# A hybrid decoder trunk: the GLU's first output block moved into the steps of the state-space layer, and its output weights stored without delay 0

## The chip, the cores and the metric

The kernel runs on 1 core of one Trainium2 chip. The metric is the device time of one execution in microseconds; the kernel before took 2366.81 us (median of 3 runs, 2366.6 to 2368.81).

## What is computed

Two layers, each followed by a dense SwiGLU network, on 16 meta tokens and 256 tokens of width 2048, all in float32. The change touches the second layer, a diagonal complex state-space layer ("S5") and the gated linear unit (GLU) behind it:

```python
def s5_mixer(u, ...):                     # u: (1, 272, 2048), 128 groups of 16 channels, 64 complex states each
    ...                                   # lb = exp(lambda*dt), bb = b scaled for the step
    bu = einsum('blgh,gph->blgp', ug, bb)
    x = associative_scan(x[t] = lb * x[t-1] + bu[t])
    y = einsum('blgp,ghp->blgh', x_re, c_re) - einsum('blgp,ghp->blgh', x_im, c_im) + d_skip * u
    g = gelu(y)
    return (g @ w_glu1) * sigmoid(g @ w_glu2)      # both weights 2048 x 2048
```

## The kernel before, in words

**Products.** A float32 product is made of three matmuls with rounded operands: the weight is split into `whi` (a copy on ACT, line 102) and `wlo` (a subtraction on DVE, line 109), the activation into `xh` and `xl`, and TensorE adds whi·xh, whi·xl and wlo·xh (`mm3`, lines 297 to 299). The class `Weights` holds the whole program's weights as one list of chunks in the order of their use. `next()` hands out a chunk and calls `pump()`, which keeps the splits up to three chunks ahead (`ahead = SA = 3`; there are `WB = 4` buffers for each part) and starts the transfers of raw chunks four ahead of the last low part (`RB = 4`, line 96, on SP's queue). A raw chunk's buffer comes free only with the low part of the chunk that was in it.

**The state-space layer.** The sequence of 272 tokens is cut into 34 pieces of T = 8 tokens. While the first dense network runs on TensorE, matrices for each of the 16 tiles of 128 channels are prepared on the other engines and written to memory: `scr[k]` (input weights, rotations and, from column `CW0` on, the output weights `wide["c"]` for the delays 0 to 8) and `taps[k]`/`toep[k]`. Each transfer of the output weights takes all nine delays; `f_y` uses the last eight, `wv = ...[:, :, 16:]`.

Then come steps, i = -1 to 23, written out by `s5_step(i)` (line 1335). In a step each stage f works on tile k = i - lag:

```python
stages = [(f_load2, 2), (f_load, -1), (f_mod, 2), (f_c, 1), (f_g3, 8), (f_g2, 7), (f_u, -1),
          (f_g1, 6), (f_scan, 3), (f_yt, 5), (f_y, 4)]
```

`f_load` and `f_load2` start three transfers (tiles `w`, `w2`, named w too in the trace, and `kt`), `f_u` scales the input, `f_c` is the matmul into `x`, `f_mod` rotates it (`rc`, `rs_`, `z`), `f_scan` scans and rotates back (`v`, `xp`), `f_y` holds the matmuls into `y`, `f_yt` transposes it (`yy`), and `f_g1`, `f_g2`, `f_g3` are the GELU, whose results are `xh[:, k]` and `xl[:, k]`, the GLU's input for channel tile k. Every engine takes its instructions in the order written.

Steps -1 to 17 run on their own. Before step 15 one `W.pump()` splits one chunk ahead. The last six steps, 18 to 23, are put into the queue that `tick()` serves after each weight chunk, between the chunks of the GLU's first block.

**The GLU.** The 16 output tiles are made in blocks of 3, 3, 3, 3, 2 and 2 (`GLU_BLOCKS`). A chunk holds two input tiles 2c and 2c+1 for one of the two weights (i = 0: w_glu2, i = 1: w_glu1) and a block's output columns; 16 chunks make a block, and each output tile needs 6 matmuls of 256 columns per chunk. A block has one PSUM bank per output tile and weight. `th` is the sigmoid's tanh; `gate` multiplies; `osq` gathers squares for the norm that follows. After the first block the PSUM and SBUF of the steps are given back.

Of the kernel before, what the change touches and what calls it, by code (L numbers as in the profile page):

```python
# [10 lines left out]
F32 = mybir.dt.float32  # L11
# [20 lines left out]
T = 8  # L32
# [108 lines left out]
def trunk(  # L141
# [5 lines left out]
    nc = tc.nc  # L147
# [56 lines left out]
    plan_ffn(0)  # L204

    GLU_ORDER = [(c, i) for c in range(6) for i in range(2)] + [(6, 0), (7, 0), (6, 1), (7, 1)]
    for a, b in GLU_BLOCKS:
        for c, i in GLU_ORDER:
            W.add(rows((s5_w_glu2, s5_w_glu1)[i][0])[:, 2 * c:2 * c + 2, a * P:b * P], (2, (b - a) * P))
    plan_ffn(1)  # L210

# [13 lines left out]
    xh = keep.tile([P, KT, NT], F32R, name="xh")  # L225
    xl = keep.tile([P, KT, NT], F32R, name="xl")
# [33 lines left out]
    psm = ps_scope.enter_context(tc.tile_pool(name="psm", bufs=3, space=PSUM))  # L260
# [6 lines left out]
    def bank():  # L267
        return psm.tile([P, 512], F32, tag="mm", name="mm")
# [416 lines left out]
    osq = Squares(KT)  # L685
# [5 lines left out]
    ps2_scope = ExitStack()  # L691
    psm = ps2_scope.enter_context(tc.tile_pool(name="psm2", bufs=8, space=PSUM))
# [114 lines left out]
    pr = par_scope.enter_context(tc.tile_pool(name="pr", bufs=1))  # L807
    XW0, EW0 = 0, 1024
    CW0 = EW0 + 8 * NCP
    SCR = CW0 + 8 * 16 * (T + 1)  # L810
    scr = [dram.tile([P, SCR], F32, name=f"scr{k}") for k in range(KT)]

    ZB = 2 * T - 1
# [34 lines left out]
    M_, A_, S_ = ALU.mult, ALU.add, ALU.subtract  # L848
# [161 lines left out]
    def par_tile(k):  # L1010
        q = slice(4 * k, 4 * k + 4)
        d = loaded.setdefault(k, {})
# [110 lines left out]
        def store():  # L1123
            w = scr[k]
            nc.sync.dma_start(out=w[:, EW0:CW0], in_=d["e"].rearrange("p i q c -> p (i q c)"))
            nc.sync.dma_start(out=w[:, CW0:], in_=wide["c"].rearrange("p i q n h -> p (i q n h)"))

        loads[k], spreads[k] = load, spread_k

# [23 lines left out]
    osq = ffn(m, Sandwich(m, 0, 1, osq, (0, 2), NT), NT)  # L1153
# [8 lines left out]
    sp_scope = ExitStack()  # L1162
    sp = sp_scope.enter_context(tc.tile_pool(name="sp", bufs=2))
    sps_scope = ExitStack()
    sps = sps_scope.enter_context(tc.tile_pool(name="sps", bufs=1, space=PSUM))
    spx_scope = ExitStack()
    spx = spx_scope.enter_context(tc.tile_pool(name="spx", bufs=3, space=PSUM))

    d0 = [sp.tile([P, 4, NC], F32, name=f"d0{a}", bufs=1) for a in range(2)]
    for a in range(2):  # L1170
# [6 lines left out]
        td[k] = {"w": w}  # L1177

    def f_load2(k):
        w = sp.tile([P, SCR - CW0], F32, tag="w2", name="w2", bufs=3)  # L1180
        nc.sync.dma_start(out=w, in_=scr[k][:, CW0:])
        kt = td[k]["kt"] = sp.tile([P, T, 8, 16], F32, tag="kt", name="kt", bufs=3)
        v = toep[k].rearrange("t n -> (t n)")[:P * KL].rearrange("(r n) -> r n", r=P)
        nc.sync.dma_start(out=kt.rearrange("r t j h -> r (t j h)"), in_=v[:, (T - 1) * P:ZB * P])
        td[k]["w2"] = w
# [47 lines left out]
    def f_y(k):  # L1233

        d = td[k]
        ps = d["ps"] = sps.tile([P, 2, 512], F32, tag="y", name="y")
        wv = d["w2"].rearrange("p (a n) -> p a n", a=8)[:, :, 16:]
        kv = d["kt"].rearrange("p t j h -> p j t h")
        for g in range(2):
            for j in range(4):  # L1240
                nc.tensor.matmul(ps[32 * j:32 * j + 32, g, :P].rearrange("c (t h) -> c t h", t=T), d["U"][:, 2 * j + g, CM:], kv[:, 2 * j + g], start=True, stop=False)
        for g in range(2):
            r = slice(64 * g, 64 * g + 64)
            for i in range(2):
                for j in range(4):
                    nc.tensor.matmul(ps[32 * j:32 * j + 32, g, :P], d["xp"][r, i, j, CM:], wv[r, 4 * i + j], start=False, stop=(i == 1))
# [30 lines left out]
    for k in range(2):  # L1277
        f_load2(k)
# [4 lines left out]
    hs = {}  # L1283

    def turn(k):

        if k % 4 == 0:
            if k == 8:

                v = sp.tile([P, SCR - CW0], F32, tag="w2", name="hs", bufs=3)[:, :4 * NT]  # L1290
                hs[2] = v.rearrange("p (s k c) -> p s k c", s=T, k=4)
            else:
                hs[k // 4] = sp.tile([P, T, 4, NC], F32, tag="hs", name="hs")
        nc.scalar.copy(hs[k // 4][:, :, k % 4], hT[:, k].rearrange("p (c s) -> p s c", s=T))
# [6 lines left out]
    def read_u(g):  # L1301
        nc.sync.dma_start(out=m_flat[:, 4 * NT * g:4 * NT * (g + 1)], in_=ub[g])

    for k in range(KT + 2):
# [14 lines left out]
        if k == KT + 1:  # L1319
# [34 lines left out]
    ps2_scope = ExitStack()
    mr = m[:, :, :NREAL]

    osq = Squares(KT, cols=NREAL)
    ths = {}
    for a, b in GLU_BLOCKS:
        n = b - a  # L1360
        p2 = [bank()[:, :NREAL] for _ in range(n)]
        p1 = [bank()[:, :NREAL] for _ in range(n)]
        now = a == 0 or b == KT
        if b == KT:
            drain()

        def gate(o, a=a, p1=p1):
            tt(mr[:, a + o], p1[o], ths[a][:, o], M_)
            osq.add(mr[:, a + o])
        for c, i in GLU_ORDER:  # L1370
            hi, lo = W.next()
            if c == 7 and i == 1:
                ts(th[:, :n], th[:, :n], 0.5, 0.5, M_, A_)
                if b == KT:
                    warm(AF.Sqrt)
            for o in range(n):
                for k in range(2):
                    kt = 2 * c + k
                    mm3((p2, p1)[i][o], hi[:, k, o * P:(o + 1) * P], lo[:, k, o * P:(o + 1) * P],
                        xh[:, kt, :NREAL], xl[:, kt, :NREAL], kt == 0, kt == KT - 1)  # L1380
                if c == 7 and i == 1 and now:
                    gate(o)
            if c == 7 and i == 0:
                if a == 0:
                    th = sp.tile([P, SCR - CW0], F32, tag="w2", name="th", bufs=3)[:, :3 * NREAL].rearrange("p (o n) -> p o n", o=3)
                else:
                    th = sg.tile([P, 3, NREAL], F32, tag="th", name="th")
                ths[a] = th
# [5 lines left out]
        if a == 0:
            drain()
            psg_scope.close()
            sps_scope.close()
            sp_scope.close()
            sg = ctx.enter_context(tc.tile_pool(name="sg", bufs=2))
            psm = ps2_scope.enter_context(tc.tile_pool(name="psm3", bufs=8, space=PSUM))  # L1400
# [116 lines left out]
```

## Time and profile before

| | |
|---|---|
| runs | 2366.6, 2366.81, 2368.81 us; median 2366.81 |
| the profiled execution | 2366.55 us, of which the span from the first to the last instruction is 2364.6 us |
| busy, share of the span | PE 97%, DVE 60%, ACT 44%, POOL 26% |
| chain that ended last | PE 90%, DVE 5%, DMA, POOL, ACT and issue 1% each |
| mean granted TensorE clock | 0.977 of 2.4 GHz |
| transferred | 463.02 MB, mean 196 GB/s |

PE is busy through nearly the whole span. The page cuts the span into 40 slices of 59 us: in all but a few, PE is at nine tenths and the clock at full. The steps of the state-space layer lie in slices 23 and 24 (counted from 1).

### The profile page before, as it was taken

The numbers are of one execution on the slowest core, as the hardware profiler recorded it, in microseconds if no ns is written. First come the engines' busy times: TensorE is split into PE (matmuls) and PEld (weight loads), VectorE is DVE, ScalarE is ACT, GpSimd is POOL, SyncE is SP. The second block draws the span as 40 slices with busy tenths as digits, with TensorE's granted clock in tenths as the row PEclk, the third lists the DMA queues.
The fourth block names the chain that finished last, engine by engine and source line by source line (L and its number), as shares of the span: only waits on it lengthen the run. The fifth ranks groups of instructions, "written<-read, shape, count | busy, mean of one in ns | idle before, by whom it ended". The sixth has DMA issues, their size and how long they took to land.

```text
span 2364.6 us, 46794 instructions
## 1 busy us (share of the span) xinstructions
PE 2301.9 (97%) x18838; PEld 2207.0 (93%) x18838; DVE 1409.7 (60%) x2056; ACT 1043.6 (44%) x1582; POOL 611.9 (26%) x811
## 2 busy tenths in 40 slices
PE   8999999999999999999999789999999999999998
PEld 7999999999999999999999569998998999989996
DVE  6555556585755666656755695558555465545565
ACT  5434444553443443333444554446444444434443
POOL 2000001148665667547402350105000000000002
PEclk9999999999999999999999759999999999999999
DMA  6555555456777777777765885555665666655654
GB/s 172 143 152 153 155 151 171 139 155 189 245 235 227 237 228 245 229 229 218 255 212 166 295 312 179 184 176 147 182 201 202 183 184 178 205 184 177 193 192 156
DMA packets 391548, 463.02 MB, mean 196 GB/s; under 512 B 68596, under 2 KB 323092, under 8 KB 391188
## 3 DMA queue, kind: packets, MB, share of 16 engines
q1 hardware_dynamic: 391104, 459.97, 62.9%
q8 instruction: 147, 2.41, 0.4%
q14 instruction: 69, 0.57, 0.1%
q10 hardware_dynamic: 228, 0.08, 0.0%
HBM read 432.37 MB, written 43.32 MB: 201 GB/s over the span
## 4 chain that ended last, share of the span: by engine, by line
PE 90%; DVE 5%; DMA 1%; POOL 1%; ACT 1%; issue 1%; SPq 0%; DVEq 0%; POOLq 0%; ACTq 0%
PE mm L297 23%; PE mm L299 23%; PE mm L298 23%; PE mm L776 5%; PE mm L1443 3%; PE mm L1444 3%; PE mm L1442 3%; DVE wlo L109 1%; PE mm L754 1%; DVE v L1226 1%; PE mm L1062 1%; PE mm L761 1%; PE mm L1079 0%; DMA w<-scr 0%; POOL ct L843 0%
## 5 line engine op out<-in xcount | busy, mean ns | idle before, releaser
L109 DVE TENSOR_TENSOR wlo<-raw,whi 128x768 fp32r<-128x768 f32 (+2 forms) x891 | 945.7, 1074 | 505.2 <-ACT whi L102 497.8
L102 ACT CAST whi<-raw 128x768 fp32r<-128x768 f32 (+2 forms) x891 | 774.1, 884 | 829.1 <-PE mm L298 455.0
L299 PE MATMUL mm<-xh,wlo 128*128 128x272 f32 (+1 forms) x3544 | 1015.7, 287 | 5.5 <-DVE wlo L109 5.5
L297 PE MATMUL mm<-xh,whi 128*128 128x272 f32 (+1 forms) x3544 | 1020.2, 288 | 0.6 <-DVE m L843 0.6
L298 PE MATMUL mm<-xl,whi 128*128 128x272 f32 (+1 forms) x3544 | 1010.0, 285 | 0.0
L299 PEld LDWEIGHTS mm<-xh,wlo 128*128 128x128 f32 x3544 | 670.0, 189 | 7.6 <-DVE wlo L109 7.5
L297 PEld LDWEIGHTS mm<-xh,whi 128*128 128x128 f32 x3544 | 671.3, 189 | 5.3 <-issue 2.8
L298 PEld LDWEIGHTS mm<-xl,whi 128*128 128x128 f32 x3544 | 670.0, 189 | 0.0
L297 PE MATMUL mm<-ah,whi 128*128 128x272 f32 x944 | 274.1, 290 | 0.5 <-ACT m L678 0.5
L299 PE MATMUL mm<-ah,wlo 128*128 128x272 f32 x944 | 273.5, 290 | 0.0
L298 PE MATMUL mm<-al,whi 128*128 128x272 f32 x944 | 271.9, 288 | 0.0
L843 POOL TENSOR_TENSOR m<-m,gb 128x512 f32<-128x512 f32 x8 | 12.1, 1511 | 710.2 <-ACT mm L1456 693.9
L297 PEld LDWEIGHTS mm<-ah,whi 128*128 128x128 f32 x944 | 177.8, 188 | 1.6 <-ACT whi L102 0.8
L299 PEld LDWEIGHTS mm<-ah,wlo 128*128 128x128 f32 x944 | 178.1, 189 | 0.1
L298 PEld LDWEIGHTS mm<-al,whi 128*128 128x128 f32 x944 | 178.2, 189 | 0.0
L314 POOL TENSOR_TENSOR sqacc<-sqacc,sq 128x272 f32<-128x272 f32 (+1 forms) x81 | 85.3, 1053 | 243.3 <-ACT sq L309 241.5
L1443 PE MATMUL mm<-wlo,ah 128*128 128x512 f32 x352 | 137.4, 390 | 1.0 <-DVE wlo L109 1.0
L1442 PE MATMUL mm<-whi,ah 128*128 128x512 f32 x352 | 138.0, 392 | 0.0
L1444 PE MATMUL mm<-whi,al 128*128 128x512 f32 x352 | 137.3, 390 | 0.0
L843 POOL TENSOR_TENSOR bc<-ct,ct 128x64 f32<-128x64 f32 (+2 forms) x128 | 91.3, 733 | 73.1 <-PE mm L1079 69.3
L785 DVE TENSOR_TENSOR gs<-mm,r 128x272 f32<-128x272 f32 (+1 forms) x82 | 35.6, 434 | 107.2 <-PE mm L299 107.2
L582 POOL TENSOR_TENSOR z<-c,x 128x272 f32<-128x272 f32 x8 | 6.3, 783 | 289.8 <-DVE x L575 192.8
(437 smaller groups left out, 2411.4 us busy)
## 6 DMA issues: line engine op xcount, KB each, us to landing
raw<-in_ffn_w_gate_dram SPq DMA_DIRECT2D x224, 384.0 KB, 3.8
raw<-in_ffn_w_up_dram SPq DMA_DIRECT2D x224, 384.0 KB, 4.1
raw<-in_ffn_w_down_dram SPq DMA_DIRECT2D x168, 512.0 KB, 4.8
raw<-in_ab_w_in_dram SPq DMA_DIRECT2D x90, 512.0 KB, 4.1
raw<-in_s_w_glu_dram SPq DMA_DIRECT2D x64, 384.0 KB, 3.7
raw<-in_ab_w_o_dram SPq DMA_DIRECT2D x32, 512.0 KB, 4.5
toep<-taps SPq DMA_DIRECT2D x16, 960.0 KB
w<-scr SPq DMA_DIRECT2D x16, 672.0 KB, 7.6
```

Of the source, the lines that this page charges most:

```text
L102: self.nc.scalar.copy(hi[:, :n], self.raw[i][:, :n])
L109: self.nc.vector.tensor_tensor(lo[:, :n], raw[:, :n], hi[:, :n].bitcast(F32), op=ALU.subtract)
L297: nc.tensor.matmul(ps, hi, bh, start=first, stop=False)
L298: nc.tensor.matmul(ps, hi, bl, start=False, stop=False)
L299: nc.tensor.matmul(ps, lo, bh, start=False, stop=last)
L314: eng.tensor_tensor(self.acc[:, :self.cols], self.acc[:, :self.cols], sq[:, :self.cols], op=ALU.add)
L776: nc.tensor.matmul(pss[o], w[:, k, o * P:(o + 1) * P], xx[:, k, :cols], start=(k == 0 and w is hi and xx is xh), stop=False)
L785: nc.vector.tensor_tensor(gs[:, o, :cols], pss[o], r["r"][:, :cols], op=ALU.mult)
L843: (eng or V).tensor_tensor(o, a, b, op=op)
L1442: nc.tensor.matmul(pss[a], ah[:, kt, ts_], hi[:, k], start=(kt == 0), stop=False)
L1443: nc.tensor.matmul(pss[a], ah[:, kt, ts_], lo[:, k], start=False, stop=False)
L1444: nc.tensor.matmul(pss[a], al[:, kt, ts_], hi[:, k], start=False, stop=(kt == kts - 1))
```

## The change

1. The GLU's blocks become 4, 3, 3, 2, 2 and 2 output tiles, and the first block's chunks come in the order (c, 0), (c, 1) for c = 0 to 7.
2. The first block of four tiles is computed inside the steps. `s5_step(i, also)` calls `also()` right behind `f_g3`; it issues one chunk of the block (24 matmuls) as soon as input tile 2c+1 is made, that is one in each of the steps 9 to 23, and one behind them. All steps now run on their own: none is interleaved with a later block.
3. Four more PSUM banks (`psb`) hold the block, two output tiles to a bank; the pool of `x` goes from three banks to two.
4. The pump before step 15 goes; behind step 1 there is one that splits four chunks ahead.
5. Behind the block its gating is done at once in two pieces per operation, and all eight banks go to the next block.
6. The output weights are stored without delay 0: 1024 columns a partition in place of 1152, written from eight pieces of 128 columns (512 bytes) per partition.

```diff
-GLU_BLOCKS = [(0, 3), (3, 6), (6, 9), (9, 12), (12, 14), (14, 16)]
+GLU_BLOCKS = [(0, 4), (4, 7), (7, 10), (10, 12), (12, 14), (14, 16)]
...
+    GLU_FIRST = [(c, i) for c in range(8) for i in range(2)]
     for a, b in GLU_BLOCKS:
-        for c, i in GLU_ORDER:
+        for c, i in GLU_FIRST if a == 0 else GLU_ORDER:
...
-    SCR = CW0 + 8 * 16 * (T + 1)
+    SCR = CW0 + P * T
...
-            nc.sync.dma_start(out=w[:, CW0:], in_=wide["c"].rearrange("p i q n h -> p (i q n h)"))
+            nc.sync.dma_start(out=w[:, CW0:].rearrange("p (a n) -> p a n", a=8), in_=wide["c"].rearrange("p i q n h -> p (i q) (n h)")[:, :, 16:])
...
-    spx = spx_scope.enter_context(tc.tile_pool(name="spx", bufs=3, space=PSUM))
+    spx = spx_scope.enter_context(tc.tile_pool(name="spx", bufs=2, space=PSUM))
+    psb = psb_scope.enter_context(tc.tile_pool(name="psb", bufs=4, space=PSUM))
...
-    def s5_step(i):
+    def s5_step(i, also):
         for f, lag in stages:
             k = i - lag
             if ahead.get(f, 0) <= k < KT:
                 f(k)
-    for i in range(-1, KT + 2):
-        if i == KT - 1:
+            if f is f_g3:
+                also()
+    nb = GLU_BLOCKS[0][1]
+    pb = [[psb.tile([P, 512], F32, tag="g", name="g") for _ in range(nb // 2)] for _ in range(2)]
...
+    def first_block(c, i):
+        hi, lo = W.next()
+        for o in range(nb):
+            for k in range(2):
+                kt, ps = 2 * c + k, half(i, o)
+                for w, v in ((hi, xh), (hi, xl), (lo, xh)):
+                    nc.tensor.matmul(ps, w[:, k, o * P:(o + 1) * P], v[:, kt, :NREAL],
...
+    def some(i):
+        if first and 2 * first[0][0] + 1 <= i - 8:
+            first_block(*first.popleft())
+    for i in range(-1, KT + 8):
+        s5_step(i, lambda: some(i))
+        if i == 1:
+            W.ahead = WB
             W.pump()
-        s5_step(i)
+            W.ahead = SA
...
-    for i, pause in zip(range(KT + 2, KT + 8), (0, 2, 2, 1, 1, 1)):
-        queues[1].extend([[]] * pause + [[lambda i=i: s5_step(i)]])
...
+    while first:
+        first_block(*first.popleft())
...
+    for o in range(0, nb, 2):
+        nc.scalar.activation(th[:, o:o + 2], pb[0][o // 2].rearrange("p (o n) -> p o n", o=2), AF.Tanh, scale=0.5)
+    W.pump()
+    ts(th, th, 0.5, 0.5, M_, A_)
+    for o in range(0, nb, 2):
+        tt(mr[:, o:o + 2], pb[1][o // 2].rearrange("p (o n) -> p o n", o=2), th[:, o:o + 2], M_)
+    for o in range(nb):
+        osq.add(mr[:, o])
```

DVE, one of the steps 11 to 14 (`rc` and `rs_` first the rotation of `x`, then of `v`; the row number behind a name is a buffer's). Before:

```order
L843 TENSOR_TENSOR rc<-x,w 128x272
L843 TENSOR_TENSOR rs__16953<-x,w 128x272
L846 SCALAR_TENSOR_TENSOR xl<-yq,xh 128x8x32
L846 SCALAR_TENSOR_TENSOR yq<-yq,yy 128x256
L843 TENSOR_TENSOR m<-m,r_u 128x8x34
L1226 SCALAR_TENSOR_TENSOR v<-d_16125,z 128x136 x2
L843 TENSOR_TENSOR rc<-v,w 128x272
L843 TENSOR_TENSOR rs__16990<-v,w 128x272
L1252 STREAM_TRANSPOSE yy<-y 128x256
```

With the change:

```order
L845 TENSOR_TENSOR rc<-x,w 128x272
L845 TENSOR_TENSOR rs__17130<-x,w 128x272
L848 SCALAR_TENSOR_TENSOR xl<-yq,xh 128x8x32
L109 TENSOR_TENSOR wlo_17160<-raw_16059,whi_17048 128x1024
L848 SCALAR_TENSOR_TENSOR yq<-yq,yy 128x256
L845 TENSOR_TENSOR m<-m,r_u 128x8x34
L1231 SCALAR_TENSOR_TENSOR v<-d_16129,z 128x136 x2
L845 TENSOR_TENSOR rc<-v,w 128x272
L845 TENSOR_TENSOR rs__17197<-v,w 128x272
L1257 STREAM_TRANSPOSE yy<-y 128x256
```

One low part of 1024 columns has come in between `xl` and `yq`; the rest of the step is as it was.

SP's queue around the steps 1 and 2, where the last input pieces are written (`ub<-hs`) and the loads of the steps begin. Before:

```order
L1299 DMA ub_4569<-hs 16x8x136 x8
L1176 DMA w<-scr_4496 128x1344
L1302 DMA m<-ub_4568 128x1088
L1176 DMA w<-scr_4497 128x1344
L1181 DMA w_16404<-scr_4495 128x1152
L1184 DMA kt<-toep_4527 128x1024
```

With the change:

```order
L1304 DMA ub_4569<-hs 16x8x136 x8
L96 DMA raw_16346<-in_s_w_glu_dram 128x2x512
L96 DMA raw_16348<-in_s_w_glu_dram 128x2x512
L1181 DMA w<-scr_4496 128x1344
L1307 DMA m<-ub_4568 128x1088
L1181 DMA w<-scr_4497 128x1344
L1186 DMA w_16423<-scr_4495 128x1024
L1189 DMA kt<-toep_4527 128x1024
```

Two raw chunks of GLU weights now stand ahead of the fourth `w`, and the output weights' transfer is shorter by 128 columns.

PE, the last matmuls into `y` (tile 15, end of step 19) and the beginning of step 20's chunk, into `g`:

```order
L1246 MATMUL y<-kt,m 32x128 x8
L1251 MATMUL y<-w_17667,xp 32x128 x16
L1361 MATMUL g<-xh,whi_17758 128x256
L1361 MATMUL g<-xl,whi_17758 128x256
L1361 MATMUL g<-xh,wlo_17835 128x256
```

From here PE has only chunks of the first block, 24 such matmuls each; before, the last matmuls into `y` stood between chunks of 18 matmuls into `mm`.

## Rows read from the trace of the kernel before

**Rows 1.** The page, 40 slices: granted clock, DMA share.
```profile
PEclk9999999999999999999999759999999999999999
DMA  6555555456777777777765885555665666655654
```
**Rows 2.** Stretch: PE, PEld, DVE, ACT, POOL busy; clock, DMA share, GB/s.
```profile
1360.00:1380.00 20.00, 16.37 (x334) 12.62 (x330) 19.58 (x41) 11.55 (x33) 12.61 (x21) 0.50 0.98 374
```
**Rows 3.** DVE in order of time: start us, duration, line, instruction.
```profile
1366.95 0.40 DVE L843 TENSOR_TENSOR rc<-x,w 128x272 f32<-128x272 f32 x1
...
1371.88 0.40 DVE L843 TENSOR_TENSOR rc<-x,w 128x272 f32<-128x272 f32 x1
...
1391.55 1.16 DVE L109 TENSOR_TENSOR wlo<-raw,whi 128x768 fp32r<-128x768 f32 x1
1392.63 0.43 DVE L843 TENSOR_TENSOR rc<-x,w 128x272 f32<-128x272 f32 x1
...
1409.67 0.45 DVE L1252 STREAM_TRANSPOSE yy<-y 128x256 f32<-128x256 f32 x1
```
**Rows 4.** PE in order of time, one of the steps at half clock.
```profile
1369.15 1.93 PE L1200 MATMUL x<-m,w 128*64 128x34 f32 x32
1372.01 1.08 PE L1241 MATMUL y<-kt,m 128*32 128x128 f32 x16 [0.93 <-DVE yy L1252]
1373.02 1.13 PE L1246 MATMUL y<-w,xp 64*32 64x128 f32 x32
```
**Rows 5.** PE in order of time, the GLU from its first to its last matmuls.
```profile
1409.27 0.41 PE L297 MATMUL mm<-xh,whi 128*128 128x256 f32 x1
...
1409.91 0.42 PE L297 MATMUL mm<-xh,whi 128*128 128x256 f32 x1
...
1412.49 0.65 PE L1241 MATMUL y<-kt,m 128*32 128x128 f32 x16
...
1413.69 0.39 PE L297 MATMUL mm<-xh,whi 128*128 128x256 f32 x1
...
1447.99 0.36 PE L297 MATMUL mm<-xh,whi 128*128 128x256 f32 x1 [0.61 <-DVE m L843]
...
1596.16 0.28 PE L299 MATMUL mm<-xh,wlo 128*128 128x256 f32 x1
```
**Rows 6.** DVE's groups, 1700 to 2300 us: count, busy us, mean ns.
```profile
L109 DVE TENSOR_TENSOR wlo<-raw,whi 128x768 fp32r<-128x768 f32 x179 | 169.9, 956 | 131.4 <-ACT whi L102 131.0
L109 DVE TENSOR_TENSOR wlo<-raw,whi 128x1024 fp32r<-128x1024 f32 x66 | 81.0, 1250 | 54.9 <-ACT whi L102 54.7 <-PE mm L1443 0.2
```
**Rows 7.** ACT's groups, whole span: the cast of a 1024-column chunk.
```profile
L102 ACT CAST whi<-raw 128x1024 fp32r<-128x1024 f32 x290 | 298.6, 1050 | 259.8 <-PE mm L298 125.5 <-DMA raw<-in_ffn_w_down_dram 67.8 <-PE mm L1444 46.5
```
**Rows 8.** SP's queue: the load of `w` for tile 3.
```profile
1335.99 0.44 SPq L1176 DMA_DIRECT2D w<-scr  x1
```
**Rows 9.** PE and DVE, first steps: idle before, and its releaser.
```profile
1355.01 1.93 PE L1200 MATMUL x<-m,w 128*64 128x34 f32 x32 [1.90 <-DMA w<-scr]
1334.69 0.44 DVE L843 TENSOR_TENSOR rc<-x,w 128x272 f32<-128x272 f32 x1 [1.33 <-PE x L1200]
```
**Rows 10.** Busy time in stretches of 4 us, columns as in rows 2.
```profile
472.00:476.00 4.00, 3.25 (x25) 2.92 (x23) 3.95 (x6) 2.49 (x7) 4.00 (x5) 1.00 0.71 193
1344.00:1348.00 4.00, 2.67 (x96) 1.99 (x80) 3.90 (x10) 1.33 (x5) 2.51 (x6) 0.93 1.01 411
1348.00:1352.00 4.00, 3.17 (x63) 2.41 (x51) 3.10 (x8) 2.46 (x10) 2.21 (x4) 0.50 1.02 411
1352.00:1356.00 4.00, 2.10 (x56) 1.65 (x52) 3.49 (x7) 1.65 (x4) 2.56 (x5) 0.50 1.03 414
1364.00:1368.00 4.00, 3.07 (x63) 2.39 (x48) 3.90 (x9) 1.96 (x5) 2.16 (x5) 0.50 0.95 330
```
**Rows 11.** DVE in order of time: tile 15, transpose to `xl`.
```profile
1423.13 0.45 DVE L1252 STREAM_TRANSPOSE yy<-y 128x256 f32<-128x256 f32 x1
...
1436.31 0.68 DVE L846 SCALAR_TENSOR_TENSOR xl<-yq,xh 128x256 fp32r<-128x256 f32 x1
```

More of the change, by code (lines that the diff above doesn't have):

```diff
@@ L1166, in trunk @@
     spx_scope = ExitStack()
-    spx = spx_scope.enter_context(tc.tile_pool(name="spx", bufs=3, space=PSUM))
+    spx = spx_scope.enter_context(tc.tile_pool(name="spx", bufs=2, space=PSUM))
+    psb_scope = ExitStack()
+    psb = psb_scope.enter_context(tc.tile_pool(name="psb", bufs=4, space=PSUM))
     d0 = [sp.tile([P, 4, NC], F32, name=f"d0{a}", bufs=1) for a in range(2)]
@@ L1179, in f_load2 @@
     def f_load2(k):
-        w = sp.tile([P, SCR - CW0], F32, tag="w2", name="w2", bufs=3)
+        w = sp.tile([P, 4 * NT], F32, tag="w2", name="w2", bufs=3)[:, :SCR - CW0]
         nc.sync.dma_start(out=w, in_=scr[k][:, CW0:])
@@ L1236, in f_y @@
         ps = d["ps"] = sps.tile([P, 2, 512], F32, tag="y", name="y")
-        wv = d["w2"].rearrange("p (a n) -> p a n", a=8)[:, :, 16:]
+        wv = d["w2"].rearrange("p (a n) -> p a n", a=8)
         kv = d["kt"].rearrange("p t j h -> p j t h")
@@ L1288, in turn @@
             if k == 8:
-                v = sp.tile([P, SCR - CW0], F32, tag="w2", name="hs", bufs=3)[:, :4 * NT]
+                v = sp.tile([P, 4 * NT], F32, tag="w2", name="hs", bufs=3)
                 hs[2] = v.rearrange("p (s k c) -> p s k c", s=T, k=4)
@@ L1339, in s5_step, with half @@
                 f(k)
-    for i in range(-1, KT + 2):
-        if i == KT - 1:
+            if f is f_g3:
+                also()
+    nb = GLU_BLOCKS[0][1]
+    pb = [[psb.tile([P, 512], F32, tag="g", name="g") for _ in range(nb // 2)] for _ in range(2)]
+    def half(i, o):
+        return pb[i][o // 2][:, NREAL * (o % 2):NREAL * (o % 2 + 1)]
+    def first_block(c, i):
[5 more added lines that the diff above has]
+                    nc.tensor.matmul(ps, w[:, k, o * P:(o + 1) * P], v[:, kt, :NREAL],
+                                     start=(kt == 0 and o % 2 == 0 and w is hi and v is xh), stop=(kt == KT - 1 and w is lo), skip_group_check=True)
+    first = deque(GLU_FIRST)
+    def some(i):
[5 more added lines that the diff above has]
+            W.ahead = WB
             W.pump()
-        s5_step(i)
+            W.ahead = SA
         if i in (2, 4):
             read_u(i // 2 + 1)
-    spx_scope.close()
-    for i, pause in zip(range(KT + 2, KT + 8), (0, 2, 2, 1, 1, 1)):
-        queues[1].extend([[]] * pause + [[lambda i=i: s5_step(i)]])
-    psg_scope = ExitStack()
-    psm = psg_scope.enter_context(tc.tile_pool(name="psg", bufs=6, space=PSUM))
-    ps2_scope = ExitStack()
+    while first:
+        first_block(*first.popleft())
     mr = m[:, :, :NREAL]
@@ L1358, in trunk @@
     ths = {}
-    for a, b in GLU_BLOCKS:
+    th = sp.tile([P, 4 * NT], F32, tag="w2", name="th", bufs=3)[:, :nb * NREAL].rearrange("p (o n) -> p o n", o=nb)
+    for o in range(0, nb, 2):
[6 more added lines that the diff above has]
+        osq.add(mr[:, o])
+    psb_scope.close()
+    spx_scope.close()
+    sps_scope.close()
+    sp_scope.close()
+    sg = ctx.enter_context(tc.tile_pool(name="sg", bufs=2))
+    ps2_scope = ExitStack()
+    psm = ps2_scope.enter_context(tc.tile_pool(name="psm3", bufs=8, space=PSUM))
+    for a, b in GLU_BLOCKS[1:]:
         n = b - a
@@ L1362, in trunk @@
         p1 = [bank()[:, :NREAL] for _ in range(n)]
-        now = a == 0 or b == KT
-        if b == KT:
+        now = b == KT
+        if now:
             drain()
@@ L1373, in trunk @@
                 ts(th[:, :n], th[:, :n], 0.5, 0.5, M_, A_)
-                if b == KT:
+                if now:
                     warm(AF.Sqrt)
@@ L1383, in trunk @@
             if c == 7 and i == 0:
[L1384 to L1388, printed above, removed]
+                th = ths[a] = sg.tile([P, 3, NREAL], F32, tag="th", name="th")
                 for o in range(n):
@@ L1393, in trunk @@
             queues[0].extend([[lambda o=o, g=gate: g(o)] for o in range(n)])
[L1394 to L1400, printed above, removed]
     act_scope = ExitStack()
```

## The prediction

> **What bounds the kernel now.** I read the slices of the page first: the granted clock is at nine tenths or more everywhere but in slices 23 and 24, where it is 0.7 and 0.5 [rows 1]. These are the steps of the state-space layer. The busy times of such a stretch tell what limits it: of 20 us DVE is busy 19.58, ACT 11.55, POOL 12.61, and the clock is at 0.50, which is the 1.2 GHz level [rows 2]. PE's 16.37 us there are many small matmuls at half clock, not a bound: in order of time each step has 1.93 us into `x` and 1.08 + 1.13 us into `y`, and an idle 0.93 us that ends with DVE's transpose [rows 4]. DVE has no gaps; from one `rc<-x` to the next it takes 1371.88 - 1366.95 = 4.93 us [rows 3]. So the steps run at DVE's pace, and PE has most of its full-speed time free.
>
> Behind them the GLU is bound by PE at full clock: from the second block's first matmul at 1447.99 to the last one's end at 1596.16 + 0.28 there are 13 output tiles of 96 matmuls, 148.45 us / 1248 = 0.119 us each [rows 5]. That is the yardstick. Every chunk that PE does inside the steps is missing from this stretch, as long as the steps don't grow by as much.
>
> **The change part by part.** The sum is made against the profiled execution (2366.55 us, 0.26 below the median).
>
> *Low parts on DVE.* With three chunks split behind step 1 the pump in steps 9 and 10 finds nothing to do; from step 11 on each step holds one cast and one low part. A 1024-column low part takes 1.250 us where POOL rests, a 768-column one 0.956 [rows 6]; the one 768-column low part within the steps took 1.16, so 0.20 more, and the next instruction began 1.08 behind its start, 0.08 before its record's end [rows 3]. I take 1.25 + 0.20 - 0.08 = 1.37 us, with bounds of 1.17 (no contention) and 1.55. Eight steps, 11 to 18, are at DVE's pace: 8 x 1.37 = +11.0. The low part before step 15 goes: -1.1. Steps 11 to 14 then take 4.93 + 1.37 = 6.30 us.
>
> *Does another engine become the bound of a step?* ACT has 11.55/20 x 4.93 = 2.85 us a step, plus a cast of 1.05 [rows 2, 7]: 3.9. POOL stays at 3.1. PE at full clock: `y` took 1412.49 to 1413.69 = 1.20 us [rows 5], `x` at most its half-clock 1.93, 24 matmuls 2.86: 5.99. DMA per step: `w` 0.69, `w2` 0.52, `kt` 0.52 and a raw chunk 0.52 MB, 2.26 MB; at the 414 GB/s of a stretch in which DMA is the limit [rows 10] 5.5 us. All below 6.30, so I add nothing, but PE and DMA are close, and PE's figure needs the full clock.
>
> *The pump behind step 1.* It puts two raw chunks (2 x 0.524 MB) ahead of the fourth `w` on SP's queue, which SP reached at 1335.99 [rows 8], and two low parts ahead of DVE's first rotation, which had waited 1.33 us for PE [rows 9], so DVE would lose 2 x 1.37 - 1.33 = 1.4 us. DMA is worse: it is at its limit there, 1.03 busy at 414 GB/s [rows 10], and PE waits for `w`, 1.90 us at one step [rows 9]. So the delay of the stream passes to the steps: 1.05 MB less three transfers of `w2` that are 0.066 MB shorter each, 0.85 MB / 414 GB/s = +2.1 us. DVE's 1.4 lies beside it. Bounds: 0 (DVE's later slack takes it) and 3.5 (both add).
>
> *The end of the steps.* Step 18 ended on DVE at 1409.67 + 0.45 = 1410.1 [rows 3]; now 1410.1 + 11.0 - 1.1 + 2.1 = 1422.1. Ten chunks are done by then. PE still has two `y` (2 x 1.20) and six chunks (6 x 24 x 0.119 = 17.1): 1441.6. The chunk (7, 0) needs tile 15's `xl`, whose chain runs on other engines beside three chunks; I take no stall. A handoff between the blocks is kept at the present 0.6 [rows 5], since the new block needs six banks, of which four were free long before. Twelve output tiles then take 148.45 x 12/13 = 137.0, up to 1579.2.
>
> *The clock.* The chunks begin at half clock, 0.213 us a matmul (1409.91 - 1409.27 for three) until it rises; in the trace of before that was within 4 us of the first GLU matmul, and the next `y` at 1412.49 is already quick [rows 5]. One start costs PE up to 17 x (0.213 - 0.119) = 1.6 us, part of it in slack. With a second such start in some step I take +1.4, with 0 and 4 as bounds: 1580.6.
>
> *The rest.* The pool of `x` with two banks: `f_c` in step i waits for the rotation of step i-1, one step earlier than now, nothing. The store of the output weights in pieces of 512 bytes: 16 stores during the first dense network, hidden by PE's work there and by chunks loaded four ahead; if each took twice its 1.3 us at 414 GB/s that would be 20 us of DMA time more in slices whose DMA share is 0.7 to 0.8 [rows 1]. I take 0, at most 2. Gating in pairs: DVE's few instructions behind chunk (7, 1), beside two chunks whose low parts are made before. Nothing.
>
> **Sum:** the GLU ended at 1596.4, now 1580.6: -15.8 us. 2366.55 - 15.8 = 2350.8, and against the median 2351.0.
>
> **The rivals.**
>
> *Slower: PE's clock falls in every step.* PE then does `y` (2.21) and `x` (1.93) and half the chunk (12 x 0.213 + 12 x 0.119 = 3.98) before it is back: 8.1 us a step, and PE is the bound of steps 9 to 18. They take 81 us in place of 58.0 (before 1366.95 - 4.93 to 1410.1, 48.1, and 11.0 - 1.1 more), +23, less the 1.4 already counted: 2372.6. It decides where the ten steps together exceed 58.0 + 17.2, that is 7.5 us a step. For it: in the steps the clock rose once, after unbroken small matmuls, 0.93 in a stretch with PE busy 2.67 of 4 us, and fell to 0.50 in the next, and with 3.07 of 4 busy it stayed at 0.50 [rows 10]. Against it: with 3.25 of 4 busy in larger matmuls the clock stayed at 1.00 [rows 10], and PE would now be busy about 5.5 of 6.3. The Trainium skill, "TensorE: Matmul & The Clock Gate", section "HAM oscillation — how this bites in real kernels", speaks for this rival: a kernel whose PE stops for data between bursts is throttled again each time and starts every burst cold; the rows show this fall once, with less work between the gaps than there will be.
>
> *The clock falls in about every third step.* 23/3 = 7.7, less 1.4: 2357.3.
>
> *DVE blocked by POOL.* A POOL instruction takes 12.61 us/21 = 0.60 on average in the steps [rows 2]. If each low part waited for a whole one, it would be 0.40 more than the 0.20 counted, 8 x 0.40 = 3.2: 2354.2. Against it speaks the 1.16 us of rows 3. The Trainium skill, "SBUF — State Buffer", section "SBUF: two separate sides", has this rule: a VectorE instruction with two SBUF inputs and a GpSimd instruction share a port pair, whoever comes first holds it for its whole instruction, and the other is blocked. By that rule alone the delay is a matter of luck; the one row lies well under the mean.
>
> *The last tile's chain is exposed.* In before it took 13.9 us from transpose to `xl` [rows 11], though with idle turns of the queue between the stages. The transpose would begin at 1422.1 + 1.20 + 2.86 + 1.20 = 1427.4, the chunk (7, 0) at 1435.9: with 13.9 PE stalls 5.4, 2356.4.
>
> That the change doesn't do what it says can be left out: the order shows a chunk behind each `x`, and nothing ahead of it that comes later than the step itself.
>
> **How the numbers follow.** The forecast 2351.0 gets 0.61, within 2346 to 2356 by the bounds of its terms; the clock in every third step 0.15, the exposed chain 0.10, POOL 0.08, the clock in every step 0.06. The range 2345 to 2361 leaves out the last and the far side of the second. No change is within 0.2% (4.7 us, about what a measurement of this kernel can tell): 2362.1 to 2371.5. The slower rival lies above it, part of the second within. Faster 0.88, same 0.05, slower 0.07.
>
> **What would show it.** Right: steps 11 to 17 with `rc<-x` starts 6 us apart and DVE without gaps; a low part of 1.3 to 1.5 us in each; PE idle before `y` about 1 us, released by `yy`; the clock at 1.00 from step 10 or 11; the first matmul of the second block at about 1442, the GLU's last at about 1580; nothing changed outside 1335 to 1600. Wrong: PE without gaps and 0.50 in the steps; waits of PE for `w` beyond step 9; a wait for `xl` before chunk (7, 0); a later first dense network.

## The result and the profile after

| | before | after |
|---|---|---|
| median of the runs in one comparison | 2367.81 us (2366.6 to 2369.53, 4 runs) | 2350.05 us (2349.37 to 2350.84, 4 runs) |
| ratio to before, 95% interval | | 0.9925 [0.9907, 0.9942] |
| the profiled execution, its span | 2366.55, 2364.6 us | 2350.18, 2348.4 us |
| mean granted clock | 0.977 | 0.986 |
| end of the GLU's last matmul | 1596.44 | 1580.31 |

The kernel is 17.8 us faster; 2351.0 was forecast. A second comparison with before gave 2350.48 us against 2366.12, 15.6 us, and 0.9935 [0.9923, 0.9948]. In the traces the GLU ends 16.1 us earlier and the span is 16.2 us shorter, while DVE's last `hn` ahead of the steps starts at 1324.54, before at 1324.58: all of the gain lies between the first step and the end of the GLU.

The granted clock in the page's 40 slices (compare [rows 1]); slices 23 and 24 are now at 0.7 and 0.8:

```profile
PEclk9999999999999999999999789999999999999999
```

The steps in stretches of 20 us (columns as in [rows 2]: PE, PEld, DVE, ACT, POOL busy us with instructions, granted clock, DMA share, GB/s):

```profile
1360.00:1380.00 20.00, 18.79 (x332) 16.00 (x336) 18.54 (x36) 10.66 (x30) 12.25 (x18) 0.68 0.88 331
1380.00:1400.00 20.00, 20.00 (x389) 17.90 (x370) 19.58 (x37) 11.92 (x29) 11.82 (x16) 1.00 0.98 364
1400.00:1420.00 20.00, 17.49 (x339) 15.00 (x338) 19.69 (x35) 13.04 (x30) 13.87 (x18) 1.00 0.94 350
```

DVE is as full as before, and PE has become full beside it in the middle stretch, at 1.00, which is the 2.4 GHz level. PE's own order in time shows how it got there, and how the GLU goes on (start, duration, engine, line, instruction, idle before with its releaser):

```profile
1344.14 1.93 PE L1205 MATMUL x<-m,w 128*64 128x34 f32 x32 [5.68 <-DMA w<-scr]
...
1369.14 0.58 PE L1361 MATMUL g<-xh,whi 128*128 128x256 f32 x1
...
1372.84 0.28 PE L1361 MATMUL g<-xh,wlo 128*128 128x256 f32 x1
...
1412.44 0.64 PE L1246 MATMUL y<-kt,m 128*32 128x128 f32 x16 [0.41 <-DVE yy L1257]
1418.19 0.64 PE L1246 MATMUL y<-kt,m 128*32 128x128 f32 x16 [1.42 <-DVE yy L1257]
1423.13 0.65 PE L1246 MATMUL y<-kt,m 128*32 128x128 f32 x16 [0.60 <-DVE yy L1257]
...
1443.94 0.36 PE L299 MATMUL mm<-xh,whi 128*128 128x256 f32 x1 [0.88 <-DVE m L845]
...
1580.03 0.28 PE L301 MATMUL mm<-xh,wlo 128*128 128x256 f32 x1
```

The first chunk begins at half clock: 16 of its 24 matmuls pass before the quick ones begin. DVE feels it at the end of step 10, where it waits for `y` and then for POOL:

```profile
1375.17 0.45 DVE L1257 STREAM_TRANSPOSE yy<-y 128x256 f32<-128x256 f32 x1 [0.48 <-PE y L1251]
1376.18 0.44 DVE L845 TENSOR_TENSOR rc<-x,w 128x272 f32<-128x272 f32 x1 [0.56 <-POOL xp L1236]
```

Step 10 takes 1376.18 - 1370.02 = 6.16 us, though it holds no low part. From there on the clock stays up. The second block's first matmul comes at 1443.94 where [rows 5] had 1447.99: the first block has a tile more and is still done 4.05 us earlier. The 12 tiles behind it take 1580.31 - 1443.94 = 136.37 us, 0.118 a matmul.

One of the steps on DVE, from `rc<-x` to `rc<-x`:

```profile
1382.40 0.40 DVE L845 TENSOR_TENSOR rc<-x,w 128x272 f32<-128x272 f32 x1
...
1383.62 1.53 DVE L109 TENSOR_TENSOR wlo<-raw,whi 128x1024 fp32r<-128x1024 f32 x1
1385.08 0.70 DVE L848 SCALAR_TENSOR_TENSOR yq<-yq,yy 128x256 f32<-128x256 f32 x1
1385.69 0.97 DVE L845 TENSOR_TENSOR m<-m,r_u 128x272 f32<-128x272 f32 x1
1386.59 0.76 DVE L1231 TENSOR_TENSOR_SCAN v<-d,z 128x136 f32<-128x136 f32 x2
1387.45 0.44 DVE L845 TENSOR_TENSOR rc<-v,w 128x272 f32<-128x272 f32 x1
...
1388.53 0.40 DVE L845 TENSOR_TENSOR rc<-x,w 128x272 f32<-128x272 f32 x1
```

and what POOL does beside it:

```profile
1383.30 0.77 POOL L1223 TENSOR_TENSOR z<-rc,rs__17130 128x136 f32<-128x136 f32 x1
1384.03 1.46 POOL L1224 TENSOR_TENSOR z<-rc,rs__17130 128x136 f32<-128x136 f32 x1
1385.45 0.91 POOL L1267 TENSOR_TENSOR yq<-yq,yy 128x256 f32<-128x256 f32 x1
1388.42 0.46 POOL L1235 TENSOR_TENSOR xp<-rc,rs__17197 128x128 f32<-128x128 f32 x1 [2.05 <-DVE rs__17197 L845]
```

The same place in a step of before, DVE:

```profile
1373.70 0.71 DVE L843 TENSOR_TENSOR m<-m,r_u 128x272 f32<-128x272 f32 x1
1374.33 1.29 DVE L1226 TENSOR_TENSOR_SCAN v<-d,z 128x136 f32<-128x136 f32 x2
1375.73 0.44 DVE L843 TENSOR_TENSOR rc<-v,w 128x272 f32<-128x272 f32 x1
```

and POOL:

```profile
1373.46 0.65 POOL L1219 TENSOR_TENSOR z<-rc,rs__16953 128x136 f32<-128x136 f32 x1
1374.07 0.92 POOL L1262 TENSOR_TENSOR yq<-yq,yy 128x256 f32<-128x256 f32 x1
```

The step takes 1388.53 - 1382.40 = 6.13 us where [rows 3] had 4.93. The low part by itself holds DVE for 1385.08 - 1383.62 = 1.46 us, and lengthens POOL's second `z` from 0.65 to 1.46. But POOL's `yq`, which in before lay beside the pair of scans, now comes later and lies beside `m`: `m` takes 0.90 to the next start in place of 0.63, the scans 0.86 in place of 1.40. Together 1.46 + 0.27 - 0.54 = 1.19 us, the growth of the step.

SP's queue at the early pump (compare [rows 8]; the first column of times is when SP reached it):

```profile
1336.47 0.92 SPq L96 DMA_DIRECT2D raw<-in_s_w_glu_dram  x2
1337.44 0.46 SPq L1181 DMA_DIRECT2D w<-scr  x1
```

### The profile page after: what moved, and what is told of

It is laid out like the page before. It is cut to its first block, busy times and chain, and to the rows that moved or that the text cites. A ratio compares the mean times of both kernels' runs of the same rounds, so it can differ in the third digit from the quotient of the medians.

```text
span 2348.4 us, 46779 instructions
## 1 busy us (share of the span) xinstructions
PE 2289.4 (97%) x18838; PEld 2198.0 (94%) x18838; DVE 1415.2 (60%) x2054; ACT 1044.4 (44%) x1580; POOL 621.3 (26%) x811
## 4 chain that ended last, share of the span: by engine, by line
PE 89%; DVE 5%; DMA 1%; ACT 1%; POOL 1%; issue 1%; SPq 0%; DVEq 0%; POOLq 0%; ACTq 0%
PE mm L299 22%; PE mm L301 22%; PE mm L300 22%; PE mm L778 5%; PE mm L1476 3%; PE mm L1475 3%; PE mm L1477 3%; DVE wlo L109 2%; PE mm L756 1%; PE g L1361 1%; DMA w<-scr 1%; PE mm L1064 1%; PE mm L763 1%; PE mm L1081 0%; POOL ct L845 0%
## 5 line engine op out<-in xcount | busy, mean ns | idle before, releaser
L301 PE MATMUL mm<-xh,wlo 128*128 128x272 f32 (+1 forms) x3416 | 976.6, 286 | 5.9 <-DVE wlo L109 5.9
L299 PE MATMUL mm<-xh,whi 128*128 128x272 f32 (+1 forms) x3416 | 980.9, 287 | 0.9 <-DVE m L845 0.9
L300 PE MATMUL mm<-xl,whi 128*128 128x272 f32 (+1 forms) x3416 | 971.1, 284 | 0.0
L301 PEld LDWEIGHTS mm<-xh,wlo 128*128 128x128 f32 x3416 | 643.4, 188 | 7.4 <-DVE wlo L109 7.4
L299 PEld LDWEIGHTS mm<-xh,whi 128*128 128x128 f32 x3416 | 644.7, 189 | 4.8 <-issue 2.4
L300 PEld LDWEIGHTS mm<-xl,whi 128*128 128x128 f32 x3416 | 643.7, 188 | 0.0
```

## The experiments

The theory: the gain is PE's work, done in steps that DVE bounds; the steps end later by one low part each and by what the early pump costs. The rivals were another cause of the gain (the shorter output weights), another bound in the steps (PE, DMA), and a cost of the early pump other than the two raw transfers.

**The shorter output weights alone** (before, and only part 6 of the change):

```diff
-    SCR = CW0 + 8 * 16 * (T + 1)
+    SCR = CW0 + P * T
...
-            nc.sync.dma_start(out=w[:, CW0:], in_=wide["c"].rearrange("p i q n h -> p (i q n h)"))
+            nc.sync.dma_start(out=w[:, CW0:].rearrange("p (a n) -> p a n", a=8), in_=wide["c"].rearrange("p i q n h -> p (i q) (n h)")[:, :, 16:])
...
-        wv = d["w2"].rearrange("p (a n) -> p a n", a=8)[:, :, 16:]
+        wv = d["w2"].rearrange("p (a n) -> p a n", a=8)
```

> The kernel before with the shorter output weights alone (stored in pieces of 512 bytes without delay 0). Theory: the stores hide under PE's work, and the loads save 0.066 MB / 414 GB/s = 0.16 us a step, which counts only in the few steps where PE waits for w: 0.3 to 0.8 us less than before, 2366.3 to 2367.5. Rival 1: the pieces cost DMA time that the first dense network feels, 1 to 2 us more than before. Rival 2: the shorter loads carry a good part of the 17 us, 3 us or more less than before.

Measured: 2365.73 us, 0.9998 [0.999, 1.0007]. That is 0.6 us under before's 2366.31 in the same comparison, within the interval: no part of the gain that can be measured lies there, and no cost of the stores in pieces of 512 bytes shows either.

**Two output tiles in the first block instead of four** (half the matmuls and half the low part in each step):

```diff
-GLU_BLOCKS = [(0, 4), (4, 7), (7, 10), (10, 12), (12, 14), (14, 16)]
+GLU_BLOCKS = [(0, 2), (2, 5), (5, 8), (8, 11), (11, 14), (14, 16)]
```

> The changed kernel with a first block of two output tiles in place of four (then 3, 3, 3, 3, 2). Theory: the gain is PE's work that the steps take in: two tiles of 96 matmuls come out of the steps, 2 x 96 x 0.119 = +22.8; low parts of 512 columns are 0.5 us shorter in eight steps, -4.4, the two early raw chunks are half as long, -1.2, and the last six chunks are shorter, at most -8.6, of which tile 15's chain leaves some 6: +11, 2358 to 2364. Rival (the gain lies in the steps running on their own, or in the shorter weights, not in how much of the GLU they hold): 2348 to 2353.

Measured: 2362.19 us, 0.9984 [0.9975, 0.9993], as expected; 3.8 us gained by the medians. The second block begins earlier than in [rows 5],

```profile
1432.16 0.36 PE L299 MATMUL mm<-xh,whi 128*128 128x256 f32 x1 [0.88 <-DVE m L845]
```

by 15.8 us, but 14 tiles are left in place of 13, and a tile costs 148.45 / 13 = 11.4 us of the stretch that PE bounds: 4.4 us gained in this trace. The steps run on their own and the output weights are shorter here too, so the gain follows PE's work in the steps and not these. This kernel also shows the falling clock of the slower rival, in a mild form (stretches of 4 us, columns as above):

```profile
1376.00:1380.00 4.00, 2.38 (x70) 1.78 (x70) 3.90 (x10) 2.15 (x8) 1.83 (x5) 0.99 1.02 408
1380.00:1384.00 4.00, 3.87 (x38) 3.60 (x39) 3.90 (x9) 1.76 (x5) 1.95 (x3) 0.58 1.04 388
1384.00:1388.00 4.00, 3.83 (x92) 3.18 (x88) 4.00 (x8) 3.15 (x9) 3.04 (x5) 1.00 1.03 366
...
1392.00:1396.00 4.00, 2.35 (x56) 1.95 (x59) 3.90 (x10) 1.97 (x5) 1.83 (x4) 1.00 1.00 356
```

Behind a stretch with PE busy 2.38 of 4 us the clock was at 0.58 for 4 us, and came back within the chunk that lies there. It did not fall each time: the last row has PE at 2.35 of 4 us, and the clock stayed at 1.00 in it and behind it.

**Two chunks in every other step** (the same work with wider gaps on PE):

```diff
-        if first and 2 * first[0][0] + 1 <= i - 8:
-            first_block(*first.popleft())
+        if i % 2 == 0:
+            for _ in range(2):
+                if first and 2 * first[0][0] + 1 <= i - 8:
+                    first_block(*first.popleft())
```

> The changed kernel with two chunks in each even step and none in the odd ones; DVE's low parts come in pairs too, and ten chunks are done by step 18 as now. Theory (DVE sets the pace, the clock needs no chunk in every step): 2349 to 2352 with the granted clock at 0.95 or more in 1376 to 1416. Rival (the clock falls in each step without a chunk): y and x of two steps at half clock, 2 x 4.1, a chunk pair of 5.7 and a start at half clock of 1.6 make 15.5 us in place of 12.3 for two steps, five pairs: 2360 to 2366, with the clock at 0.8 or less.

Measured: 2357.71 us, 0.9965 [0.9951, 0.9978], between the two: 7.7 us slower than the change as it is, by medians of two comparisons. PE before and behind the third pair:

```profile
1392.00:1396.00 4.00, 3.33 (x90) 2.69 (x88) 4.00 (x9) 2.88 (x8) 3.13 (x5) 1.00 1.00 369
1396.00:1400.00 4.00, 1.85 (x64) 1.35 (x64) 3.90 (x8) 2.56 (x7) 2.41 (x4) 0.93 1.04 415
1400.00:1404.00 4.00, 4.00 (x31) 3.93 (x31) 3.74 (x8) 2.00 (x4) 2.03 (x2) 0.50 1.02 388
1404.00:1408.00 4.00, 4.00 (x27) 4.00 (x27) 3.93 (x8) 2.85 (x8) 3.09 (x5) 0.72 1.01 383
```

and DVE's transposes behind the first pair and this one:

```profile
1384.04 0.45 DVE L1257 STREAM_TRANSPOSE yy<-y 128x256 f32<-128x256 f32 x1 [3.55 <-PE y L1251]
...
1410.66 0.45 DVE L1257 STREAM_TRANSPOSE yy<-y 128x256 f32<-128x256 f32 x1 [1.83 <-PE y L1251]
```

The clock fell behind the step without chunks, and the third pair began at half; so did the fifth, while the second and the fourth began at full clock. So neither expectation held whole: the clock falls at some of the pairs, and PE's 48 matmuls in a row hold up `y`, and with it DVE, 3.55 and 1.83 us at the first and the third pair. At the fifth, where the clock was back after six matmuls, DVE did not wait. In the changed kernel, with one chunk in each step, no such fall is seen from 1376 to the end of the GLU's first block. The Trainium skill, "TensorE: Matmul & The Clock Gate", section "HAM oscillation — how this bites in real kernels", says that a kernel which waits between bursts starts each burst cold. These rows agree for some of the bursts.

**No low parts for the first block** (`bare` names its 16 chunks; the high part is handed out in the low part's place, so that the low part's product is missing from the first four output tiles, and PE's work is the same):

```diff
+        if i in self.bare:
+            self.split[i][1] = hi
+            return
         lo = self.parts.tile([P, CHUNK], F32R, tag="wlo", name=f"wlo{i}")
```

> The changed kernel without the low parts of the first block's 16 chunks: the high part is used in their place, so the first four output tiles lack the product of the weights' low part (PE's work is the same). Theory: DVE is the bound of steps 11 to 18, and without 1.2 us a step PE is next (it took 5.3 us a step while it caught up): 8 x 0.6 to 0.9 = 5 to 7 us faster, 2343 to 2345, with PE idle gone in those steps. Rival: DMA is next at 2.26 MB / 412 GB/s = 5.5 us in steps 11 to 14: 4 to 5 us faster, and PE waits for w or w2. Second rival: something else paces the steps: less than 1.5 us faster.

Measured: 2345.57 us, 0.9911 [0.9894, 0.9928]; 4.5 us under the changed kernel's 2350.05 by the medians of two comparisons, 3.3 by their ratios to before, whose intervals overlap. PE's starts of `x` in three steps:

```profile
1379.51 1.13 PE L1210 MATMUL x<-m,w 128*64 128x34 f32 x32
...
1384.80 1.13 PE L1210 MATMUL x<-m,w 128*64 128x34 f32 x32
...
1390.08 1.13 PE L1210 MATMUL x<-m,w 128*64 128x34 f32 x32
```

and the stretches in which they lie:

```profile
1380.00:1400.00 20.00, 20.00 (x374) 18.01 (x370) 18.42 (x38) 14.37 (x36) 12.57 (x20) 1.00 0.99 363
1400.00:1420.00 20.00, 20.00 (x393) 17.49 (x386) 15.65 (x30) 13.44 (x30) 10.71 (x17) 1.00 1.01 382
```

A step takes 5.29 us, PE has no gap in 40 us, and DVE has slack: PE is the next bound, at 5.3 us. DMA may stand close behind it, at shares of 0.99 and 1.01. The theory's 5 to 7 us were somewhat too many; the amount is that of the rival with DMA, but PE does not wait for `w` or `w2` here. The second block begins at 1439.45 in place of 1443.94. Of these 4.5 us, 1.4 are there at the start of step 9 (1363.66 in place of 1365.08), so the low parts from step 9 on are worth some 3 us.

**No pump behind step 1**, and the same pump **without the raw loads**:

```diff
     for i in range(-1, KT + 8):
         s5_step(i, lambda: some(i))
-        if i == 1:
-            W.ahead = WB
-            W.pump()
-            W.ahead = SA
```

> The changed kernel without the pump behind step 1: no split and no load there, so steps 9 and 10 hold a low part each as well. Theory: the delay of the first steps goes (2.5 to 3.1 us), and two more low parts come into steps 9 and 10, 1.2 us each, of which about 1.2 lies beside PE's start at half clock, which DVE waits for in step 10 now: 1.3 to 2.0 us faster, 2348 to 2349. If low parts in the steps are free (DVE is not the bound), it is as fast as the split alone, 2347 to 2348.

Measured: 2348.16 us, 0.9923 [0.9911, 0.9936], as the theory had it.

```diff
-    def pump(self):
+    def pump(self, load=True):
...
-        self.dma(min(end, self.nl + RB))
+        if load:
+            self.dma(min(end, self.nl + RB))
...
-            W.pump()
+            W.pump(load=False)
```

> The changed kernel, but behind step 1 only the splits are made; the two raw chunks are loaded when step 9 asks for its chunk. Theory: the two raw chunks ahead of the fourth w are what makes PE wait 5.68 us for it (2.35 before), so that wait goes back to about 2.4 and DVE begins step 9 at 1362.3 to 1363 in place of 1365.1: 2.0 to 3.1 us faster than the changed kernel, 2347 to 2348. Rival: DMA owes the same bytes anyway and the steps from 9 on pay for them (DMA share there is 0.9 to 1.0): no gain, 2349.5 to 2350.5. Second rival: the two low parts on DVE make the delay: no gain either, and DVE's step 9 starts at 1365 as now.

Measured: 2346.85 us, 0.9918 [0.9904, 0.9931]. PE's first late `x`, in place of the wait of 5.68 us above:

```profile
1340.55 1.93 PE L1206 MATMUL x<-m,w 128*64 128x34 f32 x32 [2.81 <-DMA w<-scr]
```

and DVE's steps 9 and 10:

```profile
1361.68 0.40 DVE L846 TENSOR_TENSOR rc<-x,w 128x272 f32<-128x272 f32 x1
...
1366.63 0.40 DVE L846 TENSOR_TENSOR rc<-x,w 128x272 f32<-128x272 f32 x1
```

Step 9 begins at 1361.68, where the changed kernel has 1365.08 and before 1362.01: without the loads the early low parts cost nothing, and the 3.4 us hang on the two raw chunks ahead of the fourth `w`. All twelve traces bear this out. PE's fourth `x` starts between 1339.70 and 1341.55 in the kernels without these two loads, between 1343.66 and 1344.83 in those with them, and at 1342.17 with the half as long chunks of the two output tiles. One thing stays open: the kernel without low parts keeps the loads and begins step 9 at 1363.66, so with the loads in place the early low parts may add to the delay; that wasn't tried by itself. Without any pump step 9 begins at 1362.05 too, but its steps 9 and 10 hold low parts as well, and step 18 ends at 1421.04 against 1418.64.

The two kernels once more, now side by side:

> The changed kernel itself, in one job with its variants. Expected 2349 to 2351 us, ratio to before 0.992 to 0.994.

> The early splits without the two raw loads, beside the changed kernel on one chip. Theory (the two raw chunks ahead of the fourth w on SP's queue hold the whole chain of steps back until its end, where step 18's transpose came 4.4 us earlier without them, and the second block's first matmul too, 1443.94 against 1439.50): 3 to 4.5 us faster than the changed kernel. Rival (a part of it comes back later in the GLU or in the network behind it, or belonged to the job's chip): 1 to 2 us.

Measured: 2350.48 us (2349.62 to 2352.3) and 2347.67 us (2346.54 to 2348.35), 0.9935 [0.9923, 0.9948] and 0.9922 [0.9909, 0.9936] of before: 2.8 us between the medians, no overlap of the runs, between the two expectations. In the first pair of traces the second block begins 4.4 us earlier (1439.50 against 1443.94), and in the two pairs the GLU ends 4.3 and 4.8 us earlier; 1.5 to 2 us of this aren't found in the medians of these two. The executions of one kernel lie 1 to 3 us apart, and where the rest goes stays open.

**The scaling of the input on POOL**, on top of that, and in before:

```diff
-        tt(d["U"], d["U"], r_u.unsqueeze(1).to_broadcast([P, 8, NC]), M_)
+        tt(d["U"], d["U"], r_u.unsqueeze(1).to_broadcast([P, 8, NC]), M_, eng=G)
```

> As the one before, with the input's scaling (m<-m,r_u, 0.97 us of DVE in steps 11 to 17) on POOL, which idles 2.05 us a step. Theory (DVE bounds the steps at 6.13 us and PE stands next at 5.3): steps 11 to 17 take 5.3 us, PE without a gap from the first chunk on, the second block begins some 3.4 us earlier than without it, 2343 to 2344 us. Rival (POOL's scaling stands ahead of yq, whose tanh and transpose chain then comes later, and the two engines' instructions lengthen one another): steps of 5.8 us or more, at most 1 us faster, or slower.

Measured: 2346.18 us (2345.45 to 2347.67), 0.9918 [0.9904, 0.9931]; 1.5 us under the kernel without it, with runs that overlap. DVE, from the low part to the next step:

```profile
1384.19 1.50 DVE L109 TENSOR_TENSOR wlo<-raw,whi 128x1024 fp32r<-128x1024 f32 x1
1385.62 0.69 DVE L849 SCALAR_TENSOR_TENSOR yq<-yq,yy 128x256 f32<-128x256 f32 x1
1386.24 1.85 DVE L1232 TENSOR_TENSOR_SCAN v<-d,z 128x136 f32<-128x136 f32 x2
...
1389.27 0.41 DVE L846 TENSOR_TENSOR rc<-x,w 128x272 f32<-128x272 f32 x1
...
1395.47 0.40 DVE L846 TENSOR_TENSOR rc<-x,w 128x272 f32<-128x272 f32 x1
```

and POOL:

```profile
1385.99 0.96 POOL L846 TENSOR_TENSOR m<-m,r_u 128x272 f32<-128x272 f32 x1
1386.92 0.87 POOL L1268 TENSOR_TENSOR yq<-yq,yy 128x256 f32<-128x256 f32 x1
```

`m` has left DVE, and the step still takes 1395.47 - 1389.27 = 6.20 us: the scans take 1.85 us where they took 0.76, since POOL's `m` and `yq` now both lie beside them. The theory (5.3 us a step) falls, and the rival holds for the steps. What little is gained lies earlier: step 9 starts at 1359.89 in place of 1360.82 and step 11 at 1370.38 in place of 1372.52.

> Before, with the scaling on POOL and nothing else. Theory (in before DVE bounds the steps at 4.93 us, and DMA stands next: 1.8 MB a step at 414 GB/s is 4.35 us): steps 9 to 17 take 4.35 to 4.5 us, 4 to 6 us faster than before, 2360 to 2362. Rival (POOL lengthens DVE by as much as it takes off it): within 1 us of before.

Measured: 2365.07 us, 0.9994 [0.9985, 1.0003]: nothing that can be told from no change, as the rival had it. DVE's scans and the instruction behind them:

```profile
1372.77 1.57 DVE L1226 TENSOR_TENSOR_SCAN v<-d,z 128x136 f32<-128x136 f32 x2
1374.44 0.72 DVE L843 TENSOR_TENSOR rc<-v,w 128x272 f32<-128x272 f32 x1
```

The scans take 1.46 to 1.57 us there (1.29 before), the `rc<-v` behind them 0.71 or 0.72 (0.44 before), and a step 4.8 us in place of 4.93: of the 0.63 us that `m` took on DVE, some 0.5 have come back in its neighbours.

The fastest median of a kernel that computes everything is that of the one with both edits, 2346.18 us, though its runs overlap those with the first edit alone. What the kernel can do without for certain is the half of the early pump that loads.

## Why the prediction was right, point by point

- **The bound of the steps.** DVE, as forecast: `rc<-x` follows at 6.12 to 6.13 us in steps 12 to 14 without a gap. Taking the low parts away made them 5.29 us at PE's pace. The estimate of PE at 5.99 was too high: it took `x` at half clock, 1.93, and at full clock `x` takes 1.13. DMA, estimated at 5.5 us a step, held nothing up: with PE's 5.29 us steps it moved 363 to 382 GB/s and PE had no gap, though at shares of 0.99 and 1.01 it may have had little left.
- **Low parts.** 11.0 us was forecast for eight. A low part took 1.46 us to the next start, above the 1.37 and within the bounds, but the net growth of a step was 1.2 (6.13 - 4.93), since POOL's instruction moved off the scans. From the start of step 11 to the end of step 18 the eight cost (1423.07 - 1376.18) - (1410.12 - 1371.88 - 1.08) = 9.7. The term was 1.3 us too large.
- **The early pump.** +2.1 was forecast, with bounds of 0 and 3.5; step 9 came 1365.08 - 1362.01 = 3.1 later. The place and the kind were right: the two raw chunks, not the low parts by themselves, as the kernel with the low parts alone showed. The size counted their bytes (less the shorter `w2`). What the trace adds is that SP spent 0.92 us on issuing the two and reached `w` 1.45 us later than in [rows 8], 0.48 of it ahead of the two. How the rest divides wasn't tried.
- **The clock.** One start at half clock, as forecast, with 16 slow matmuls. It was counted on PE with 1.4; it showed on DVE, which waited 0.48 us for `y` at the end of step 10 and 0.56 for POOL's `xp` behind it: step 10 took 6.16 us in place of 4.93, 1.2 more (6.72 in the second trace of this kernel). There was no second start: PE made up for the late start at 5.3 us a step, and idled before `y` only from 1400 on.
- **The end of the steps** was forecast for 1422.1 and came at 1423.07: +1.0 from the pump, +1.2 from step 10 (the sum has it in the clock's term, behind this point), -1.3 from the low parts.
- **The rest.** From there to the second block 20.9 us in place of 20.1 (2.4 + 17.1 + 0.6): 0.88 in place of 0.6 at the handoff, the other 0.5 in the two `y` and six chunks. No stall for tile 15's `xl`: it was made at 1436.27 + 0.72, and PE had no gap before the handoff, so the rival of the exposed chain fell. The chain took 7.3 us from the transpose at 1429.72 where that rival took over the 13.9 of before, whose stages waited for turns of the queue. Twelve tiles took 136.4, forecast 137.0. End of the GLU 1580.3, forecast 1580.6.
- **The rivals on the clock.** Not here, but near: with half the work a step, and with the work in pairs, the clock did fall. With one chunk of 24 matmuls in each step it stayed up, and of the three grains that ran this is the only one that kept it so.
- **DVE blocked by POOL** named a contention that is there, but with too much of it: the low part took 1.53 us, 0.28 more than alone, where the forecast had 0.20 more and this rival 0.60. And the step grew by less than the low part, since the time that the engines take from each other depends on which instructions meet.

The sum was right to 0.3 us in the GLU's end because terms of about 1 us of both signs cancelled; that closeness is luck. The mechanism, and the place of each cost, are not.

## What to carry to other kernels

Where a stage is bound by another engine and PE runs it at half clock, put PE's later work into it in pieces of every step, not in bunches: here a first block with two tiles fewer was some 12 us slower, though two tiles are only 22.8 us of PE's time in the GLU, so that a tile moved into the steps cost about half of its price there (six of the block's 16 chunks come only behind step 18). Small steady pieces kept the clock up. Count what the pieces bring with them on the bound engine, and keep their prefetches off a queue whose transfers the stage is waiting for: two transfers ahead of one that is already late were worth 3 us here. Before moving work from DVE to POOL, look at what it will run beside: here it came to lie beside DVE's scans, and most of what it freed was lost again.

## What the runs showed of the hardware

- DVE and POOL lengthen one another, here by nearly as much as moving an instruction had freed. A pair of scans took 0.76 us beside a resting POOL, 1.29 beside one POOL instruction of 0.92, and beside two of 0.80 to 0.96 1.46 to 1.57 or 1.73 to 1.85, by where in them it lay. A `z` of 0.65 on POOL took 1.46 beside a low part, and the low part 1.53 in place of 1.25 [rows 6]: it began 0.45 us before the end of the first `z` and took 0.28 more, while the second `z` ended 0.34 us behind it. The Trainium skill, "SBUF — State Buffer", section "SBUF: two separate sides", says that a VectorE instruction with two SBUF inputs and a GpSimd instruction that reads SBUF exclude one another for a whole instruction. The rows fit that, with the low part held up by what was left of the first `z` and the second `z` by the low part. They don't prove it, since a record doesn't tell waiting from running slowly.
